# Second layer's experts: the 16 smallest in groups of four instead of two, and one-hot products in bursts of four

## The chip, the cores and the metric

One NeuronCore of a Trainium2 chip runs the whole program. The metric is the device time of one execution in microseconds. Three runs of the kernel before gave 2965.05 us at the median (2964.98 to 2975.44).

## The reference

The reference is a network of three layers on 512 tokens of width 1024, in float32. The first two layers (`first_block`) each end in a mixture of experts. Only the second of these is touched by the change. What it computes:

```
g_idx = argmax(h @ grp_w + grp_b)                     # one of 4 groups per token
e_logit = (h @ exp_w + exp_b)[the 8 experts of that group]
top_v, top_i = top_k(e_logit, 2)                      # two experts of 32 per token
w = g_prob * softmax(top_v)
y[e] = (silu(x[e] @ w_gate[e]) * (x[e] @ w_up[e])) @ w_down[e]     # 1024 -> 512 -> 1024
out[token] = sum over its two experts of w * y[e][token]
```

So 512 tokens make 1024 (token, expert) rows, spread unevenly over 32 experts. Every expert has three weight matrices of 2 MB in float32, 6 MB together; all 32 are read once, 192 MB.

## The kernel before

The expert stage of a layer is `moe`. A router first works out, on VectorE (DVE), each token's two experts, their weights, and each row's position within its expert. Experts 0 and 1 are always the first block. The other 30 are ranked by their number of tokens (`places`), and the list of experts in rank order (`order_list`) is written to memory, where the queue that issues the weight loads (SyncE, SP) reads it into registers (`ranked_expert`).

A block has 128 slots, one for each row of a tile. In the second layer `FIRST = 2` and `MANY = 4`: block 0 holds experts 0 and 1 with 64 slots each; blocks 1 to 4 ("singles") hold one expert each, the four with the most tokens, with 128 slots; the 26 others go in 13 pairs with 64 slots each. That is 18 blocks. The list `turn` gives the order in which they run: the first pair, then a single and three pairs by turns. Rows that don't fit into their expert's slots go to a loop (`overflow`) that stands behind block 12 in turn and whose body runs only if there is such a row.

A block runs through `expert`: its 128 rows are gathered from memory (an indirect DMA on GpSimd, POOL), transposed on TensorE (PE) into `xt`, then multiplied by gate and up (8 row chunks of 128 each, accumulated), activated, transposed into `ht`, and multiplied by down. In a pair the two experts' products stand on the two halves of PE's columns (`tile_position` 0 and 64), so that they can run at once. A float32 product shows as two instructions in the trace. The weights come in tiles of 128 x 1024 float32 (512 KB), 12 to an expert, 384 in all, through a ring of 28 buffers that are used strictly in turn (`raw`, `turn_of`): a load waits until PE is done with the tile that was there 28 tiles ago. Loads are issued by SP in the order gate of block e, down of block e-1, up of block e; PE's order is fixed by hand in the same way (`pe_turn`, `pe`).

The result of a block is added to the residual X by one-hot products: `own_parts` scales the block's output and splits it into a high and a low part, and `add_own` multiplies, for each of 8 column chunks, both parts by a one-hot matrix of the rows' tokens and adds the product to X on DVE. These are slipped in between the expert products of the next blocks: `expert` calls `hooked` after each group of loads (4 calls for gate, 4 for up, 4 for down), and each call takes one step of `add_own`, so two one-hot products over the full array.

After the last block its `add_own` is handed on to the feed-forward part of the third layer, which starts with it.

Of the kernel before, what the change touches and what calls it, by code (L numbers as in the profile page):

```python
# [14 lines left out]
I32 = DT.int32  # L15
AF = mybir.ActivationFunctionType
ALU = mybir.AluOpType
# [8 lines left out]
NE = 32  # L26
NX = 15

FIRST = (2, 2)
MANY = (8, 4)  # L30
Q_LORA, KV_LORA = 384, 256
BIG = 1 << 20
SEGS = [(0, 512), (512, 256)]
# [26 lines left out]
class Kernel:  # L60
# [607 lines left out]
    def places(self, l, pool, tt):  # L668


        V = self.nc.vector
        oh, pos, _, cnt = self.choice
        V.tensor_copy(cnt, self.pc[:, :NE])
        mk = lambda name, *s, dt=F32: pool.tile([128, *s], dt, name="p" + name)
        n1 = FIRST[l] + MANY[l]
        key = mk("key", NE)
        V.scalar_tensor_tensor(key, cnt, float(NE), self.order0[:, l], op0=ALU.mult, op1=ALU.add)
        gt, rank = mk("gt", NE, NE), mk("rank", NE)
        V.tensor_tensor(gt, key.unsqueeze(1).to_broadcast([128, NE, NE]), key.unsqueeze(2).to_broadcast([128, NE, NE]), ALU.is_gt)
        V.tensor_reduce(rank, gt, axis=AX.X, op=ALU.add)  # L680
        oxr, rk = mk("ox", tt, 2, NE), mk("rk", tt, 2)
        V.tensor_tensor(oxr, oh, rank.unsqueeze(1).unsqueeze(1).to_broadcast([128, tt, 2, NE]), ALU.mult)
        V.tensor_reduce(rk, oxr, axis=AX.X, op=ALU.add)
        g, gi, odd, slot = mk("g", tt, 2), mk("gi", 2, tt, 2, dt=I32), mk("odd", 2, tt, 2), mk("slot", tt, 2)
        V.tensor_scalar(g, rk, float(n1), 0.0, op0=ALU.subtract, op1=ALU.max)
        V.tensor_copy(gi[:, 0], g)
        V.tensor_scalar(gi[:, 1], gi[:, 0], 1, None, op0=ALU.arith_shift_right)
        V.tensor_scalar(gi[:, 0], gi[:, 0], 1, None, op0=ALU.bitwise_and)
        V.tensor_copy(odd, gi)

        V.tensor_tensor(g, rk, g, ALU.subtract)
        V.tensor_tensor(g, g, odd[:, 1], ALU.add)
        n = MANY[l] + (NE - n1) // 2
        n += n % 2
        ohb = mk("ohb", tt, 2, n)
        V.tensor_tensor(ohb, self.iota[:, FIRST[l]:FIRST[l] + n].unsqueeze(1).unsqueeze(1).to_broadcast([128, tt, 2, n]),
                        g.unsqueeze(3).to_broadcast([128, tt, 2, n]), ALU.is_equal)

        V.tensor_scalar(g, rk, float(n1), -64.0, op0=ALU.is_ge, op1=ALU.mult)
        V.scalar_tensor_tensor(g, g, 128.0, pos, op0=ALU.add, op1=ALU.is_le)  # L700
        V.scalar_tensor_tensor(slot, odd[:, 0], 64.0, pos, op0=ALU.mult, op1=ALU.add)
        V.scalar_tensor_tensor(slot, g, float(BIG), slot, op0=ALU.mult, op1=ALU.add)
        self.ranked = (gt, rank)
        return ohb, slot

    def order_list(self, l, pool, p2):

        V = self.nc.vector
        gt, rank = self.ranked
        V.tensor_tensor(gt, rank.unsqueeze(1).to_broadcast([128, NE, NE]),  # L710
                        self.iota[:, :NE].unsqueeze(2).to_broadcast([128, NE, NE]), ALU.is_equal)
        V.tensor_tensor(gt, gt, self.iota[:, :NE].unsqueeze(1).to_broadcast([128, NE, NE]), ALU.mult)
        f = p2.tile([128, NE], F32, name="pord")
        V.tensor_reduce(f, gt, axis=AX.X, op=ALU.add)
        self.order = pool.tile([1, NE], I32, name="pordi")
        V.tensor_copy(self.order, f[0:1])
        self.cap = pool.tile([128, NE], F32, name="pcap")
        V.tensor_scalar(self.cap, rank, float(FIRST[l] + MANY[l]), -64.0, op0=ALU.is_ge, op1=ALU.mult)
        light = p2.tile([128, NE], F32, name="plight")
        V.tensor_scalar(light, rank, float(FIRST[l]), -64.0, op0=ALU.is_lt, op1=ALU.mult)  # L720
        V.scalar_tensor_tensor(self.cap, self.cap, 128.0, light, op0=ALU.add, op1=ALU.add)

# [119 lines left out]
    def moe(self, l, n_tok, fg, side_work):  # L842
# [3 lines left out]
        V = nc.vector  # L846
        X = self.X
        tt = n_tok // 128
# [5 lines left out]
        with ExitStack() as st:  # L854
# [4 lines left out]
            with ExitStack() as st1:  # L859
                self.rings.append((st1.enter_context(tc.tile_pool(name=f"raw{l}", bufs=self.more_raw[l], reuse_waits="tile")), self.more_raw[l], None))  # L860
                wsp, n = self.wrings[0][:2]
                self.rings += [(wsp, n, None, "wh"), (wsp, n, None, "wl")]
                with ExitStack() as st2:
# [75 lines left out]
                    self.router(l, lt, pool, p2, n_tok)  # L939
                    oh, pos, v3, _ = self.choice  # L940
                    n1 = FIRST[l] + MANY[l]
                    nb = 1 + MANY[l] + (NE - n1) // 2

                    def lists(name, one_hot, place, bufs):
                        n = one_hot.shape[-1]
# [9 lines left out]
                    one, place, none = [p2.tile([128, tt, 2], F32, name=x) for x in ("fone", "fplace", "fnone")]  # L955
# [10 lines left out]
                    self.order_list(l, pool, p2)  # L966
                    srow, stok, swt = [lambda b, x=x, y=y: y[:, b - 1:b] if b else x for x, y in zip(first, later)]

                turn = [0]
                apart = (nb - 1 - MANY[l]) // MANY[l]  # L970
                for i in range(nb - 1 - MANY[l]):
                    single = [1 + i // apart] * (i % apart == 0 and i // apart < MANY[l])
                    turn += single + [1 + MANY[l] + i]
                pair = n1 - 2 * (1 + MANY[l])
                ranks = lambda b: [0, 1] if b == 0 else [b + 1] if b <= MANY[l] else [2 * b + pair, 2 * b + pair + 1]
                ysc = []
                with ExitStack() as st2:
                    p2 = st2.enter_context(tc.tile_pool(name=f"moee{l}", bufs=1, reuse_waits="tile"))
# [76 lines left out]
                    adds = iter(())  # L1055
# [9 lines left out]
                    for e in range(nb):  # L1065
                        if e == 0:
                            with tc.issue_after(last.ins), tc.issue_after(after_q):
                                next(ex[e])
                        else:
                            if e == own[1] and not direct:  # L1070
                                self.hook = (1, rows)
                            self.pe_turn = direct or e >= own[1]
                            next(ex[e])
                        if e + 1 < nb:
                            start(e + 1)
                        if e:
                            pss = next(ex[e - 1])
                            if direct:
                                for _ in adds:
                                    pass  # L1080
                                adds = add_own(parts_of(e - 1, pss, self.own))
                                self.hook = (1, adds)
                            elif e == own[1]:
                                mine = parts_of(e - 1, pss, p2.tile([128, n_tok], F32R, name="own", tag="ey", bufs=self.eys))
                                self.hook = (2, rows)
                            else:
                                put(e - 1, self.rows_of(p2, pss, swt(turn[e - 1])))
                                if e == own[0]:
                                    next(rows)
                        next(ex[e])  # L1090
                        if e == 2:
                            with tc.issue_after(self.split_last):
                                self.extra(pool)
                            if not direct:

                                z = p2.tile([128, 2, D], F32, name="zero", tag="yr", bufs=2)[:, 0]
                                nc.gpsimd.memset(z, 0.0)
                                for i in own:
                                    put(i, z)
                        if e == self.pause:  # L1100
                            for _ in adds:
                                pass
                            self.hook, self.pe_turn = None, False
                            self.overflow(l, n_tok, h2d, Yd, p2, xg[(e + 2) % 3], add if direct else None)
                            self.pe_last = None
                        if e >= 4:
                            for _ in range(2):
                                next(side_work, None)
# [6 lines left out]
                    if direct:  # L1115
                        adds = add_own(parts_of(nb - 1, pss, self.own, self.turn_of(self.wrings)[0]))
                    else:
                        adds = add_own(mine, parts_of(nb - 1, pss, p2.tile([128, n_tok], F32R, name="own2", tag="ey", bufs=self.eys), p2))
# [18 lines left out]
                    self.fence()  # L1137
        return s

    hook = None  # L1140

    def hooked(self):
        if self.hook:
            for _ in range(self.hook[0]):
                next(self.hook[1], None)

    def pe(self, f, *a, **kw):

# [34 lines left out]
    def expert(self, pool, l, es, x, queue=None):  # L1183
# [16 lines left out]
            else:  # L1200
                nc.scalar.activation(d, v, AF.Copy)
        yield
        parts = [(slice(0, 128), {})] if len(es) == 1 else [(slice(c, c + 64), {"tile_position": (0, c)}) for c in (0, 64)]
        h = pool.tile([128, 512], F32, name=self.uid("eh"), tag="eh", bufs=2)
        for name in ("exp_w_gate", "exp_w_up"):
            ps = self.bank()
# [1194 lines left out]
```

## Time and profile before

| | us |
|---|---|
| median of 3 runs | 2965.05 |
| profiled execution | 2964.15 |
| its span, first to last instruction | 2962.5 |
| PE busy over the span | 2758.8 (93%) |
| DVE busy | 1353.9 (46%) |
| ACT busy | 886.7 (30%) |
| POOL busy | 411.0 (14%) |
| weight tiles read by the two expert stages | 768 of 512 KB |

The profile is of one execution. PE's busy time counts matmuls that overlap as one stretch, so 93% does not say that PE runs at its peak. The second layer's experts lie between about 1278 and 1817 us of the span.

### The profile page before, as it was taken

Reading aid. Unit: us, or ns where it says so; the run is one execution under the profiler, and the core shown is the slowest. Engines: PE = TensorE matmul, PEld = TensorE weight load, DVE = VectorE, ACT = ScalarE, POOL = GpSimd, SP = SyncE. Lnnn points to the kernel's source line nnn. Section 1 sums busy time; section 2 is a strip of 40 time slices with the busy share of each in tenths; the row PEclk is TensorE's granted clock in tenths of the full one; section 3 lists DMA queues with packets and bytes.
Section 4 is the critical chain, followed back from the end, with each engine's and each line's share of the span. In section 5 each row is a group of like instructions: output and inputs, shape, how many; then the busy total and the mean of one; then the engine's idle time right before and its main releaser. Section 6 shows DMA issues by size and latency. Waiting matters only on the chain. (4 is left out here: it accounts for less than half of the span.)

```text
span 2962.5 us, 35613 instructions
## 1 busy us (share of the span) xinstructions
PE 2758.8 (93%) x12938; PEld 1803.1 (61%) x12938; DVE 1353.9 (46%) x2423; ACT 886.7 (30%) x1421; POOL 411.0 (14%) x408
## 2 busy tenths in 40 slices
PE   7989799999988999979999998999999889999998
PEld 4757644333325888833333333788888667888886
DVE  4883520000035576744333334654336777444335
ACT  3563211110103577300000002223225666332223
POOL 1772210000001000010000000650003230000000
PEclk9999899999999999989999999999999999999999
DMA  7666599999994101389999894343334422333331
GB/s 258 210 204 211 219 389 406 399 398 404 398 411 170 63 26 60 115 351 403 372 394 362 335 417 145 104 119 103 97 93 126 135 51 82 97 96 100 93 94 63
DMA packets 207685, 634.63 MB, mean 214 GB/s; under 512 B 29808, under 2 KB 39120, under 8 KB 206736
## 3 DMA queue, kind: packets, MB, share of 16 engines
q1 hardware_dynamic: 194208, 598.89, 55.7%
q0 software_dynamic: 13296, 33.41, 3.1%
q8 instruction: 103, 1.69, 0.2%
q14 instruction: 78, 0.64, 0.1%
HBM read 619.12 MB, written 26.71 MB: 218 GB/s over the span
## 5 line engine op out<-in xcount | busy, mean ns | idle before, releaser
L1152 PE MATMUL ps<-raw,xt 128*64 128x512 f32 (+1 forms) x2048 | 593.4, 608 | 12.0 <-DMA raw<-exp_w_up 8.4
L169 PE MATMUL ps<-Hh,wh 128*128 128x512 f32 (+1 forms) x1320 | 495.2, 381 | 3.5 <-ACT Hh L262 2.1
L171 PE MATMUL ps<-Hh,wl 128*128 128x512 f32 (+1 forms) x1320 | 495.7, 377 | 2.9 <-DVE wl L91 2.9
L170 PE MATMUL ps<-Hl,wh 128*128 128x512 f32 (+1 forms) x1320 | 497.9, 378 | 0.2 <-DVE Hl L263 0.2
L89 ACT ACTIVATE wh<-raw 128x1024 fp32r<-128x1024 f32 (+1 forms) x224 | 231.6, 1040 | 582.5 <-PE ps L170 477.6
L1152 PEld LDWEIGHTS ps<-raw,xt 128*64 128x64 f32 (+1 forms) x2048 | 189.1, 148 | 329.9 <-issue 269.4
L91 DVE TENSOR_TENSOR wl<-raw,wh 128x1024 fp32r<-128x1024 f32 (+1 forms) x224 | 276.2, 1237 | 204.8 <-ACT wh L89 204.5
L1152 PE MATMUL ps<-raw,ht 128*64 128x512 f32 (+1 forms) x1024 | 281.1, 597 | 29.1 <-DVE ht L1225 26.3
L169 PEld LDWEIGHTS ps<-Hh,wh 128*128 128x128 f32 x1320 | 248.5, 189 | 67.9 <-issue 5.0
L170 PEld LDWEIGHTS ps<-Hl,wh 128*128 128x128 f32 x1320 | 249.2, 189 | 55.4 <-issue 4.2
L171 PEld LDWEIGHTS ps<-Hh,wl 128*128 128x128 f32 x1320 | 248.5, 189 | 51.0 <-DVE wl L91 3.8
L1218 DVE TENSOR_TENSOR eh<-ps,eh 128x512 f32<-128x512 f32 x38 | 26.3, 692 | 417.5 <-PE ps L1152 377.9
L1152 PEld LDWEIGHTS ps<-raw,ht 128*64 128x64 f32 (+1 forms) x1024 | 100.2, 146 | 188.9 <-issue 146.3
L1029 DVE SCALAR_TENSOR_TENSOR X<-ps,mod,X 128x512 f32<-128x512 f32 (+1 forms) x160 | 116.7, 736 | 190.2 <-PE ps L1152 190.1
L1216 ACT ACTIVATE eh<-ps 128x512 f32<-128x512 f32 x38 | 22.7, 597 | 478.3 <-PE ps L1152 478.2
L413 POOL TENSOR_TENSOR cg<-cg,cp 128x798 f32<-128x798 f32 x60 | 121.8, 2030 | 95.7 <-ACT cp L412 87.6
L985 POOL DMA_INDIRECT xg<-h2d,stok x36 | 36.2, 1005 | 515.4 <-PE ps L1152 464.2
L169 PE MATMUL ps<-Gh,wh 128*128 128x512 f32 x256 | 101.1, 395 | 0.0
L171 PE MATMUL ps<-Gh,wl 128*128 128x512 f32 x256 | 101.1, 395 | 0.0
L170 PE MATMUL ps<-Gl,wh 128*128 128x512 f32 x256 | 101.1, 395 | 0.0
L1571 DVE TENSOR_TENSOR fs<-ps,fs 128x512 f32<-128x512 f32 x44 | 30.4, 691 | 142.6 <-PE ps L171 141.9
L1152 PEld LDWEIGHTS ps<-own,ysh 128*128 128x128 f32 x152 | 28.4, 187 | 95.7 <-issue 93.0
(741 smaller groups left out, 4153.7 us busy)
## 6 DMA issues: line engine op xcount, KB each, us to landing
raw<-exp_w_gate SPq DMA_DIRECT2D x256, 512.0 KB
raw<-exp_w_up SPq DMA_DIRECT2D x256, 512.0 KB
raw<-exp_w_down SPq DMA_DIRECT2D x256, 512.0 KB
raw<-ffn_w SPq DMA_DIRECT2D x132, 512.0 KB
raw<-mod_w SPq DMA_DIRECT2D x96, 512.0 KB
X<-xT SPq DMA_DIRECT2D x16, 384.0 KB
raw<-w_in_ab SPq DMA_DIRECT2D x12, 512.0 KB
yr<-yd POOLq DMA_DIRECT2D x6, 1024.0 KB, 8.3
```

The source lines that it names most:

```text
L89: self.nc.scalar.activation(dst.hi, src, AF.Copy)
L91: self.split_last = eng.tensor_tensor(dst.lo, src, dst.hi.bitcast(F32), ALU.subtract).ins
L169: mm(ps, a.hi, b.hi, start=start, stop=False)
L170: mm(ps, a.hi, b.lo, start=False, stop=False)
L171: mm(ps, a.lo, b.hi, start=False, stop=stop)
L413: nc.gpsimd.tensor_tensor(a, a, t, ALU.add)
L985: nc.gpsimd.indirect_dma_start(out=x, out_offset=None, in_=h2d, in_offset=bass.IndirectOffsetOnAxis(ap=stok(turn[e]), axis=0), bounds_chec ...
L1029: V.scalar_tensor_tensor(xs, ps[:, :c], self.mcol(l, 5, k, i), xs, op0=ALU.mult, op1=ALU.add)
L1152: i = f(*a, **kw).ins
L1216: nc.scalar.activation(h, ps, AF.Silu)
L1218: nc.vector.tensor_tensor(h, ps, h, ALU.mult)
L1571: V.tensor_tensor(s, ps, s, ALU.mult)
```

## The change

The second layer gets a third kind of block. `FEW = (0, 16)`: of the ranked experts the last 16 get 32 slots each and run four to a block, on quarters of PE's columns (`tile_position` 0, 32, 64 and 96). The ten experts of ranks 6 to 15 stay in 5 pairs. That makes 1 + 4 + 5 + 4 = 14 blocks. `places` works out the new slots, `order_list` the new number of slots per expert for the overflow test. The order in `turn` becomes: the first pair, then a four and a single, four times, then the five pairs. In the first layer `FEW` is 0, and its blocks and their order are as before.

The hook that adds the one-hot products takes two steps at every second call instead of one step at each: four one-hot products in a row, half as often.

```diff
+FEW = (0, 16)
 # places
+        n2 = NE - FEW[l]
         V.tensor_scalar(g, rk, float(n1), 0.0, op0=ALU.subtract, op1=ALU.max)
+        if FEW[l]:
+            f, fi, quarter = mk("f", tt, 2), mk("fi", 2, tt, 2, dt=I32), mk("quarter", 2, tt, 2)
+            V.tensor_scalar(f, rk, float(n2), 0.0, op0=ALU.subtract, op1=ALU.max)
+            V.tensor_tensor(g, g, f, ALU.subtract)
+            V.tensor_copy(fi[:, 0], f)
+            V.tensor_scalar(fi[:, 1], fi[:, 0], 2, None, op0=ALU.arith_shift_right)
+            V.tensor_scalar(fi[:, 0], fi[:, 0], 3, None, op0=ALU.bitwise_and)
+            V.tensor_copy(quarter, fi)
...
+        if FEW[l]:
+            V.tensor_tensor(g, g, f, ALU.subtract)
+            V.tensor_tensor(g, g, quarter[:, 1], ALU.add)
-        n = MANY[l] + (NE - n1) // 2
+        n = MANY[l] + (n2 - n1) // 2 + FEW[l] // 4
...
+        if FEW[l]:
+            V.tensor_scalar(f, rk, float(n2), -32.0, op0=ALU.is_ge, op1=ALU.mult)
+            V.tensor_tensor(g, g, f, ALU.add)
...
+        if FEW[l]:
+            V.scalar_tensor_tensor(slot, quarter[:, 0], 32.0, slot, op0=ALU.mult, op1=ALU.add)
 # order_list
+        if FEW[l]:
+            V.tensor_scalar(light, rank, float(NE - FEW[l]), -32.0, op0=ALU.is_ge, op1=ALU.mult)
+            V.tensor_tensor(self.cap, self.cap, light, ALU.add)
 # moe
-                    nb = 1 + MANY[l] + (NE - n1) // 2
+                    n2 = NE - FEW[l]
+                    nb = 1 + MANY[l] + (n2 - n1) // 2 + FEW[l] // 4
...
+                one = list(range(1, 1 + MANY[l]))
+                two = list(range(1 + MANY[l], 1 + MANY[l] + (n2 - n1) // 2))
                 turn = [0]
-                apart = (nb - 1 - MANY[l]) // MANY[l]
-                for i in range(nb - 1 - MANY[l]):
-                    single = [1 + i // apart] * (i % apart == 0 and i // apart < MANY[l])
-                    turn += single + [1 + MANY[l] + i]
-                pair = n1 - 2 * (1 + MANY[l])
-                ranks = lambda b: [0, 1] if b == 0 else [b + 1] if b <= MANY[l] else [2 * b + pair, 2 * b + pair + 1]
+                for b in [*range(1 + MANY[l] + len(two), nb), *two]:
+                    turn += [one.pop(0), b] if one and (not FEW[l] or len(turn) > 1) else [b]
+                turn = [*turn[:-1], *one, turn[-1]]
+                pair, four = n1 - 2 * (1 + MANY[l]), n2 - 4 * (nb - FEW[l] // 4)
+                ranks = lambda b: ([0, 1] if b == 0 else [b + 1] if b <= MANY[l] else
+                                   [2 * b + pair + i for i in range(2)] if b in two else [4 * b + four + i for i in range(4)])
...
-                                self.hook = (1, adds)
+                                self.hook = (2, adds, 2)
 # hooked
-            for _ in range(self.hook[0]):
-                next(self.hook[1], None)
+            n, g, *every = self.hook
+            self.beat += 1
+            if self.beat % (every or [1])[0] == 0:
+                for _ in range(n):
+                    next(g, None)
 # expert
-        parts = [(slice(0, 128), {})] if len(es) == 1 else [(slice(c, c + 64), {"tile_position": (0, c)}) for c in (0, 64)]
+        n = 128 // len(es)
+        parts = [(slice(c, c + n), {} if n == 128 else {"tile_position": (0, c)}) for c in range(0, 128, n)]
```

## Rows read from the trace of the kernel before

**Rows 1.** Timeline of ACT and PE, end of the stage: start us, us, engine, line.
```profile
1816.53 1.52 ACT L1012 ACTIVATE wh<-ps,swt 128x512 fp32r<-128x512 f32 x2 [19.63 <-PE ps L1152]
1824.78 1.05 PE L169 MATMUL ps<-Hh,wh 128*128 128x512 f32 x2
```

**Rows 2.** Windows: window, length, busy PE PEld DVE ACT POOL, granted clock, DMA share, GB/s.
```profile
1278.00:1797.00 519.00, 490.79 (x1954) 190.71 (x1956) 183.13 (x321) 35.42 (x53) 16.86 (x17) 0.99 0.97 381
1676.00:1780.00 104.00, 99.50 (x398) 36.75 (x396) 36.65 (x56) 7.29 (x11) 0.00 (x0) 1.00 1.03 416
1300.00:1340.00 40.00, 37.73 (x146) 16.87 (x144) 13.56 (x21) 2.57 (x4) 2.96 (x3) 1.00 1.03 416
1260.00:1280.00 20.00, 5.43 (x32) 4.82 (x30) 18.36 (x82) 1.92 (x4) 2.72 (x2) 0.63 0.51 180
840.00:860.00 20.00, 15.04 (x48) 4.27 (x45) 4.80 (x8) 0.00 (x0) 1.75 (x3) 0.91 1.03 414
```

**Rows 3.** Waits of PE, 1281 to 1820: total us, times, longest us.
```profile
PE ps L1152 <- DVE ht L1225: 25.5, 18, 1.9
```

**Rows 4.** Waits of SP's queue, 1280 to 1800: total us, times, longest us.
```profile
SPq L133 <- PE ps L1152: 194.3, 164, 19.2
...
SPq L793 <- DVE xli L780: 1.9, 1, 1.9
```

**Rows 5.** Chain of waits, two pairs: start us, us, what.
```profile
1729.70 27.22 PE ps L1152 x112
...
1760.00 27.22 PE ps L1152 x112
```

**Rows 6.** Timeline of PE: a down projection, pair chunks, single chunks.
```profile
1402.04 7.09 PE L1152 MATMUL ps<-raw,ht 128*64 128x512 f32 x32 [1.50 <-DVE ht L1225]
...
1411.44 1.94 PE L1152 MATMUL ps<-raw,xt 128*64 128x512 f32 x8
...
1413.97 1.94 PE L1152 MATMUL ps<-raw,xt 128*64 128x512 f32 x8
...
1418.94 1.88 PE L1152 MATMUL ps<-raw,xt 128*128 128x512 f32 x4
...
1421.12 1.88 PE L1152 MATMUL ps<-raw,xt 128*128 128x512 f32 x4
```

**Rows 7.** Timeline of SP's queue: the issue of tiles (xN of them).
```profile
1276.27 1.95 SPq L133 DMA_DIRECT2D raw<-exp_w_gate  x4
...
1294.78 9.00 SPq L133 DMA_DIRECT2D raw<-exp_w_gate  x8
...
1343.05 10.67 SPq L133 DMA_DIRECT2D raw<-exp_w_up  x8
...
1641.67 2.62 SPq L133 DMA_DIRECT2D raw<-exp_w_gate  x4
...
1683.34 9.08 SPq L133 DMA_DIRECT2D raw<-exp_w_gate  x8
...
1774.34 9.69 SPq L133 DMA_DIRECT2D raw<-exp_w_down  x8
1794.46 46.19 SPq L133 DMA_DIRECT2D raw<-ffn_w  x8
```

**Rows 8.** Four-quarter products elsewhere: those running at 24.2 us; timeline at 1830.80.
```profile
L362 PE MATMUL ps<-raw,sc x4: 1062/1062/1062, 24.2 to 24.2; 128*32 128x512 f32 x4
...
1830.80 1.06 PE L1152 MATMUL ps<-x,gs 128*32 128x512 f32 x6
```

**Rows 9.** Timeline of DVE: the ordered list is written.
```profile
1275.61 0.17 DVE L716 CAST pordi<-pord 1x32 int32<-1x32 f32 x1
```

**Rows 10.** DMA queues, 1280 to 1800: packets, MB, share of 16 engines.
```profile
DMA packets 55603, 197.87 MB, mean 381 GB/s; under 512 B 7367, under 2 KB 7367, under 8 KB 55570
...
q0 software_dynamic: 2448, 4.02, 2.1%
```

**Rows 11.** SP at the branch of the overflow loop: both layers, first and last start.
```profile
L794 SPq COMPARE_BRANCH x2: 45/49/53, 674.2 to 1621.8; - x2
```

**Rows 12.** The page's first line.
```profile
span 2962.5 us, 35613 instructions
```

More of the change, by code (lines that the diff above doesn't have):

```diff
@@ L1138, in moe @@
         return s
-    hook = None
+    hook, beat = None, 0
     def hooked(self):
         if self.hook:
-            for _ in range(self.hook[0]):
-                next(self.hook[1], None)
+            n, g, *every = self.hook
[3 more added lines that the diff above has]
+                    next(g, None)
     def pe(self, f, *a, **kw):
```

## The prediction

> **What bounds the kernel now.** I first looked for the stretch that the edit touches: the second layer's experts, from the first gathered block near 1278 us to the eviction of the last one at 1816.53 [rows 1]. The windows view gives PE busy 490.79 of 519 us and a mean of 381 GB/s over it [rows 2]. So two resources are nearly full, and the question is which one waits for the other. The waits view settles it: PE's longest wait in the stretch is for DVE's copy of `ht`, 25.5 us in 18 pieces, once per block [rows 3], and no expert tile appears among PE's waits; SP, which issues the tiles, waits 194.3 us for PE to free buffers [rows 4]. PE is late, the DMA is held back. The chain of waits says the same: two pairs in a row start their third piece at 1729.70 and 1760.00, and what lies between is PE plus about 3 us of DVE at the hand-over [rows 5]. A pair costs 30.3 us.
>
> A sum over blocks confirms it. On the PE timeline a chunk of a pair (8 instructions of 64 columns, two running at once, plus one one-hot visit) takes 1413.97 - 1411.44 = 2.53 us, a chunk of a single 1421.12 - 1418.94 = 2.18 us; a down projection takes 7.09 us for 32 instructions, so one slot is 0.433 us [rows 6]. A single is 8 x 2.18 + 7.1 + 3.3 (transposes and hand-over) = 27.8 us. Before: 14 pairs x 30.3 + 4 singles x 27.8 = 535 us; seen, from the restart near 1283 to 1816.53, 533 us.
>
> How fast could the DMA go? While SP was issuing without a pause, 72 tiles of 512 KB (nine groups of eight) went from 1683.34 to 1774.34 [rows 7]: 91.0/72 = 1.264 us each, at 416 GB/s and a DMA share of 1.03. The stretch 1300 to 1340 has the same 416 GB/s and 1.03 at an earlier, different place [rows 2], so I take that as the ceiling. A pair's 24 tiles need 30.3 us, which equals PE's pace; a single's 12 need 15.2 us against PE's 27.8. The lost DMA time is in the singles and in a stop before 1641.67, where SP waited 19.2 us for PE [rows 4, 7].
>
> **The change part by part.**
>
> *18 blocks become 14.* The 26 experts of rank 6 and up were 13 pairs; now there are 5 pairs and 4 fours. The order is pair, then four and single four times over, then five pairs. All 384 tiles are still loaded. A four runs the same number of array slots as a pair if four 32-column products run at once. The trace has that form elsewhere: at 24.2 us four products of 128x32 are in flight together, and at full clock six such records span 1.06 us, which is two slots and the tail of one [rows 8]. So a chunk of a four is 4 slots, 1.73 us, and its block about 29 us of PE, while its 48 tiles take 48 x 1.264 = 60.7 us. PE's total becomes about 6 x 29.4 + 4 x 27.8 + 4 x 29 = 404 us. PE leaves the path and the DMA takes it.
>
> *DMA sum.* The first load of the second block is issued at 1276.27, when 16 of the 384 tiles have been issued [rows 7]; that waits for the ordered list, written at 1275.61 [rows 9]. Remaining: 368 x 1.264 = 465.2 us. Gathers share the engines: the software queue has 2.1% of the 520 us window, 10.9 us [rows 10], and moves the same 1024 token rows afterwards, so I keep 10.9. First landing about 2 us after issue (estimate; the wait pieces on the DMA are 1 to 2 us). Last tile: 1276.3 + 2 + 465.2 + 10.9 = 1754.4, or 1.29 us a tile with the gathers in it.
>
> *PE behind the last tile.* After a four PE is level with the tiles. The last single puts it behind by at most 27.8 - 15.5 = 12 us, spread over its neighbours some 9; each of the five pairs takes 24 x 1.29 = 31.0 us of DMA against 29.4 of PE and gives back 1.6. That leaves 2 us, plus a few at the overflow branch: 6 us. Bounds: 2 (the last chunk alone) and 10 (nothing given back).
>
> *Bursts.* A visit costs 2.53 - 4 x 0.433 = 0.80 us in a pair but 2.18 - 4 x 0.433 = 0.45 in a single, whose products use the whole array like the one-hot ones; the 0.35 us is the change of array form [rows 6]. Four visits fewer per block save 1.4 us of PE; the second addition to X at the hand-over (0.75 us on DVE, partly overlapped) gives back about 0.5. So a pair is 29.4. It matters only at the end, as above; 14 blocks instead of 18 also drop 64 one-hot products, off the path now.
>
> *The overflow branch* stands after block 12 in turn in both versions. SP passes it at 1621.8 without stopping [rows 11]; its first load behind it then waited the 19.2 us, because the body that is not run takes 12 of the 28 buffers in turn, so that load needs the tile 16 back, not 28 back, to be done. With SP waiting for buffers all along, PE was then nearly the whole ring behind. With PE under 10 us (8 tiles) behind, this stall goes: 0 us, at worst 5. What is late next is the DMA itself.
>
> *Longer router.* `places` has eleven more small DVE instructions and `order_list` two, near 0.17 us each with issue [rows 9]. Most of them lie beside or behind the list that SP waits for; SP then reads four registers per four instead of two. On the path: 0.5 us, between 0 and 13 x 0.17 = 2.2. PE's first product moves by as much, hidden by the loads. SP's read of the overflow list stands in the same queue and waited 1.9 us [rows 4]; beside the tiles in flight it costs 0, at worst 5.
>
> *Does a token fall out of 32 slots?* Routing the reference's drawn inputs, the 16 smallest experts of layer two hold at most 30 tokens, ranks 6 to 15 at most 49. The overflow body stays unrun.
>
> *The tail.* The first FFN tiles are issued at 1794.46, 22 us before PE is done [rows 1, 7]; now they land only a few us before. Their two splits may then stand in the way of the last evictions: 1.5 us, between 0 and 4. Layer one and all else are unchanged.
>
> *Sum.* PE ends at 1754.4 + 6 + 0.5 = 1761 instead of 1816.5: -55.5; tail +1.5: -54. The profiled execution took 2964.15 us (span 2962.5 [rows 12]) and would take 2910; the median, 2965.05, is 0.9 above it: **2911 us**. With all low ends (no gather cost, PE 2 behind, no tail): 1276.3 + 2 + 465.2 + 2 = 1745.5, -71, 2894. With a tile at the pace between 1294.78 and 1343.05 (36 tiles in 48.3 us, 1.34 each, gathers within) [rows 7]: 368 x 1.34 = 493, PE end 1777.5 + 0.5, tail 4: 2931.
>
> **The rivals.**
> *The clock falls in the fours.* PE now waits for tiles. When it was busy 5.43 of 20 us the granted clock was 0.63, at 15.04 of 20 it was 0.91 [rows 2]. In a four, products start tile by tile: two slots after each of the first three tiles, four after the last, 4.3 of 5.2 us per chunk, so I expect near 1. At the lower level (1.2 GHz, a slot twice as long) a four's PE time is about 12 x 3.5 + 8 x 1.2 + 4 = 56 us, still under its loads, but the singles then find no slack, and each four and single together need 56 + 27.8 = 84 us against 77: four times 7 is 28 us, 2939. The Trainium skill ("TensorE: Matmul & The Clock Gate", Loop structure matters more than you think) speaks for this: waiting for a DMA between bursts of products makes PE run slow. By that rule the sum would be these 2939 us; the trace's 0.91 lies nearer to mine.
> *The DMA does not go faster.* If four experts' streams kept the mean of 381 GB/s, the window's 197.87 MB [rows 10] would take 519 us as now; only PE's part behind the last tile shrinks: 1278 + 519 + 6 = 1803, 2953 us. Against it: 416 GB/s over 104 us, with pairs.
> *Slower: quarters one after another.* If each of the four products of a row chunk waited for the one before, a chunk would be 16 slots, 6.9 us, a four 12 x 6.9 + 8 = 91 us, over its 61 us of loads; then PE binds again: 4 x 91 + 4 x 27.8 + 6 x 29.4 = 652 us, end 1936, 3085 us. It decides from two at a time downward: at two a four is 50 us and stays under its loads. Against it: the four records in flight together.
>
> **How the numbers follow.** Forecast 0.79, slow clock 0.12, no faster DMA 0.06, serial quarters 0.03. About 0.5% (15 us) is what a measurement can tell from no change, so faster means under 2950: forecast, slow clock and a third of the third case, 0.93; same 0.04; slower 0.03. The range runs from 2894 to 2938: the forecast with both ends and most of the slow clock's case.
>
> **What would show it.** Right: in the changed profile PE's waits in the stretch are for `exp_w_*` tiles, SP's for PE nearly vanish, DMA stays at 1.03 and 416 GB/s from 1280 to about 1750, four 128x32 records start together, and the FFN's first product moves from 1824.78 [rows 1] to about 1771. Wrong: GB/s near 390 with PE waiting (ceiling misread), a granted clock under 0.8 in the fours, 6 to 7 us per chunk of a four, or a long SP wait at the branch.

## The result and the profile after

The changed kernel takes 2923.02 us (median of 4 runs, 2919.81 to 2926.05) against 2965.51 (4 runs, 2964.98 to 2975.44): a ratio of 0.9849, 95% interval 0.9826 to 0.9872. The prediction was 2911, within 2894 to 2938. The sign and the mechanism came out; 12 us of the gain did not.

All of the gain lies in the second layer's expert stage. Its end on ACT and the FFN's first product, which stood at 1816.53 and 1824.78 [rows 1], in the timelines of the changed kernel (start us, us, engine, line):

```profile
1775.22 1.53 ACT L1037 ACTIVATE wh<-ps,swt 128x512 fp32r<-128x512 f32 x2 [18.95 <-PE ps L1180]
...
1784.13 1.05 PE L171 MATMUL ps<-Hh,wh 128*128 128x512 f32 x2
```

That is -41.3 us where -55.5 was forecast, and 0.7 us given back in the tail where 1.5 was. From the FFN on both kernels take the same: 2962.5 - 1824.78 = 1137.7 us before, 2921.4 - 1784.13 = 1137.3 after.

The waits of SP's queue in the changed kernel, 1280 to 1790 (total us, times, longest us):

```profile
SPq L135 <- DMA raw<-exp_w_down: 94.8, 124, 2.8
SPq L135 <- DMA raw<-exp_w_gate: 89.4, 116, 2.0
SPq L135 <- DMA raw<-exp_w_up: 88.2, 118, 2.1
SPq L135 <- PE ps L1180: 13.1, 43, 0.8
```

SP used to wait 194.3 us for PE [rows 4] and 117 us for its own transfers; now it waits 272 us for its own transfers and 13 for PE, and the 19.2 us at the overflow branch are gone. The bound has moved from PE to the loads, as forecast. A four whose tiles are all there, on PE's timeline:

```profile
1305.21 7.07 PE L1180 MATMUL ps<-raw,xt 128*32 128x512 f32 x64 [0.35 <-DVE xt L1224]
```

These are 64 quarter products, 16 slots if four run at once: 7.07/16 = 0.442 us a slot, against 0.433 [rows 6]. So the rival of serial quarters is out. The windows view (length, busy PE PEld DVE ACT POOL, granted clock, DMA share, GB/s):

```profile
1300.00:1340.00 40.00, 36.74 (x191) 11.64 (x188) 6.68 (x10) 3.38 (x5) 1.97 (x2) 1.00 1.03 408
1340.00:1400.00 60.00, 54.21 (x225) 20.45 (x225) 25.79 (x67) 2.57 (x4) 1.97 (x2) 0.97 1.03 407
1460.00:1560.00 100.00, 90.20 (x367) 31.59 (x366) 25.10 (x41) 4.54 (x7) 2.96 (x3) 1.00 1.03 408
1676.00:1740.00 64.00, 60.48 (x270) 24.20 (x268) 24.19 (x37) 3.95 (x6) 0.00 (x0) 1.00 1.02 407
```

In these windows, three of which hold fours, the granted clock is 0.97 to 1.00, so the slow clock is out too. The last column is what was not expected: the same DMA share of 1.02 to 1.03 as before, but 407 to 408 GB/s and not 416 [rows 2].

### The profile page after: what moved, and what is told of

Read it like the earlier page. It is cut to its first block, busy times and chain, and to the rows that moved or that the text cites. A ratio compares the mean times of both kernels' runs of the same rounds, so it can differ in the third digit from the quotient of the medians.

```text
span 2921.4 us, 35291 instructions
## 1 busy us (share of the span) xinstructions
PE 2709.3 (93%) x12826; PEld 1783.5 (61%) x12826; DVE 1310.1 (45%) x2372; ACT 878.8 (30%) x1409; POOL 405.8 (14%) x404
## 3 DMA queue, kind: packets, MB, share of 16 engines
q1 hardware_dynamic: 194208, 598.89, 55.5%
## 5 line engine op out<-in xcount | busy, mean ns | idle before, releaser
L1180 PE MATMUL ps<-raw,xt 128*64 128x512 f32 (+2 forms) x2048 | 571.4, 607 | 21.5 <-DMA raw<-exp_w_up 13.8
L1180 PEld LDWEIGHTS ps<-raw,xt 128*64 128x64 f32 (+2 forms) x2048 | 181.4, 141 | 364.0 <-issue 237.5
L1180 PE MATMUL ps<-raw,ht 128*64 128x512 f32 (+2 forms) x1024 | 275.1, 616 | 28.9 <-DVE ht L1254 20.6
L1180 PEld LDWEIGHTS ps<-raw,ht 128*64 128x64 f32 (+2 forms) x1024 | 93.9, 142 | 192.7 <-issue 130.3
L1054 DVE SCALAR_TENSOR_TENSOR X<-ps,mod,X 128x512 f32<-128x512 f32 (+1 forms) x128 | 88.1, 729 | 152.8 <-PE ps L1180 152.8
L422 DVE SCALAR_TENSOR_TENSOR cv<-U,cw,cv 128x512 f32<-128x512 f32 x120 | 76.2, 635 | 3.1
```

Of the source, the lines that this page charges most:

```text
L422: V.scalar_tensor_tensor(s, u, cw[:, g, j:j + 1], s, op0=ALU.mult, op1=ALU.add)
L1054: V.scalar_tensor_tensor(xs, ps[:, :c], self.mcol(l, 5, k, i), xs, op0=ALU.mult, op1=ALU.add)
L1180: i = f(*a, **kw).ins
```

## The experiments

Whole times of one kernel scatter by 5 to 15 us, and the second block's first tile is issued anywhere between 1276 and 1284 in these profiles, in both kernels (1267 in e7, for a reason told there). So each run is also judged by its **stage length**: from that issue to the first eviction of the last block. It is 1816.53 - 1276.27 = 540.3 us before [rows 1, 7] and 1775.22 - 1279.63 = 495.6 us after. Ratios are to the kernel before.

**Is 416 GB/s the kernel's or that execution's?** The kernel before again, unchanged.

> The kernel before, unchanged, profiled beside the other runs of this batch. It tells whether the 416 GB/s that its first profile showed at 1300 to 1340 and 1676 to 1780 us belong to the kernel or to that execution; the changed kernel's profile has 407 GB/s in the same stretches at the same DMA share of 1.02. If the ceiling differs from execution to execution (or from chip to chip): the two stretches show some other rate here, and the other profiles of this batch show the same one in their starved stretches, within 3 GB/s. If the ceiling is lower in the changed kernel because of what it does (four experts' tiles in flight side by side, another order of experts): 416 again here and 407 again in the changed kernels of this batch.

2969.74 us, stage length 540.0. The windows view:

```profile
1300.00:1340.00 40.00, 38.60 (x149) 16.65 (x145) 10.38 (x15) 3.85 (x5) 1.98 (x2) 1.00 1.03 417
1676.00:1740.00 64.00, 61.00 (x240) 23.65 (x238) 20.74 (x32) 3.95 (x6) 0.00 (x0) 1.00 1.03 417
```

The rate belongs to the kernel. The changed kernels of the same batch show 408 in the first window (e2 and e4, the latter with pairs there, not fours), so four experts side by side are not the reason either.

**Bursts taken back, and bursts alone.** In the changed kernel, and in the kernel before:

```
-  self.hook = (2, adds, 2)
+  self.hook = (1, adds)        # e2; e3 is the reverse, in the kernel before
```

> The changed kernel with the one-hot products given out one visit per chunk again, as in the kernel before; fours stay. A visit costs a block of column groups about 0.35 us more than a single's, so 4 x 0.35 = 1.4 us of PE per block, less some 0.5 us of the second addition: 0.9 us. Theory A (the loads set the pace until the last tile, and PE ends some 8 us behind it, a lag made by the last single and worked off in the last five pairs at 31.6 us of loads against 29 of PE): only the last single and the five pairs count, 6 x 0.9 to 6 x 1.4, so +5 to +8 us against the changed kernel, 2928 to 2931. Theory B (PE sets the pace all along): 14 x 0.9 = +13 us or more. Theory C (the loads alone set the end): 0 to +1 us.

> The kernel before with bursts alone: two visits on every second chunk, pairs and singles as they were, 18 blocks. There PE sets the pace, so each of the 14 pairs should save what a burst saves on PE. By the prediction's 0.9 us (four visits fewer x 0.35, less 0.5 at the hand-over) 14 x 0.9 = -13 us, about 2953; if nothing is given back at the hand-over, 14 x 1.4 = -20 us, 2946. Rival: the one-hot visits cost PE nothing that isn't hidden, or the pairs are held by the loads (24 x 1.264 = 30.3 us, which equals PE's pace), so 0 to -3 us, 2962 to 2965. What it shows is the part of the -42 us that the edit of the bursts alone brings.

Without bursts 2922.69 us, ratio 0.9846 (0.9830 to 0.9861), the same as with them; stage length 498.2. Theory C in the whole time, half of A in the stage: the bursts carry next to nothing here. Alone they bring 0.9968 (0.9956 to 0.9981), -9.5 us, stage length 535.0; -13 was the prediction's price. In the profiled run, too, the stage is only 5.0 us shorter than in e1. The last pairs of the kernel before give nothing: their gate tiles are issued 1719.01 - 1688.84 = 30.17 us apart without bursts (e1) and 1718.39 - 1688.23 = 30.16 with them (e3), the pace of 24 tiles at 417 GB/s.

**A four last.** 

```
+  turn = [0, *range(5, 10), 1, 10, 2, 11, 3, 12, 4, 13]
```

> The changed kernel with its blocks in another order: the five pairs come right behind block 0 and the stage ends with single, four, single, four, ... and last a four, whose tiles take twice PE's time. Theory A (PE ends 8 us behind the last tile because singles make a lag that the pairs work off only slowly): PE ends about 2 us behind, so -6 us against the changed kernel; up to 3 us of it lost, because a four's last chunk needs four tiles: -3 to -6, 2917 to 2920. Theory B (PE sets the pace): 0. A loss of over 3 us would mean that order itself costs something, for example the overflow block's place among the tiles.

2919.83 us, ratio 0.9839 (0.9824 to 0.9854), too close to 0.9849 to call; stage length 494.7, -0.9. Theory A wanted -3 to -6. So whatever lies behind the last tile, little of it is a lag that singles make and pairs work off; how much is read from the tiles' completions below.

**What the tile buffers' addresses do.** One more difference between the kernels touches a transfer: where it lands. Tiles go through 28 buffers in turn. By the program's own allocation, 17 of them moved from 87552 to 87456, since the router's lists ahead of them have one column a block, rounded up to 14 instead of 18, and so became 96 bytes smaller; the other 11 start 32 above a multiple of 64 in both kernels. Three paddings of the changed kernel, and one of the kernel before:

```
+  if l == 1: pool.tile([128, 24], F32, name="pad")   # e5: 96 bytes; e6: [128, 8], 32 bytes
                                                       # e8: 32 bytes, kernel before
   # e7: 8 floats in front of every ring, 24 more in layer one, 16 more in layer two
```

> The changed kernel with 96 unused bytes per partition in front of the second layer's 17 extra tile buffers. The longer list code, whose tiles are allocated ahead of them, is 96 bytes smaller than before, so those 17 of the 28 buffers that expert tiles go through moved from address 87552 to 87456 (from a multiple of 256 to 32 above a multiple of 64); the other 11 start 32 above a multiple of 64 in both kernels. This puts the 17 back to 87552 and changes nothing else. Theory A (a tile costs more DMA time where its buffer does not start on a boundary): the starved stretches at 1300 to 1340 and 1676 to 1740 show 416 to 417 GB/s instead of 407 to 408, a tile 1.26 instead of 1.285 us, 368 x 0.025 = -9 us, 2914. Theory B (the lower rate comes from more tiles in flight, or from PE, DVE and the DMA meeting otherwise): 408 GB/s and 2923 us as in the changed kernel.

> The same with 32 unused bytes: the 17 buffers start at 87488, a multiple of 64 but 192 above a multiple of 256. If a boundary of 64 bytes is what counts: 416 GB/s and 2914 us, as in the run with 96 bytes. If it is one of 256: the rate stays at 405 to 409, 2923 us. The Trainium skill (DMA: Bandwidth & Descriptors, How a descriptor splits into AXI transactions) says that a transaction must start from a 256-byte boundary and that the bytes between that boundary and the start still cost beats of 32 bytes: by it 4096 bytes would take 128 beats at a multiple of 256, 133 at the changed kernel's 87456, 134 here, 135 in the other 11 buffers; that is 130.8 on the mean before, 133.8 after and 134.4 here, so 405 GB/s here by the 407 of after.

> The changed kernel with unused bytes ahead of every ring of tile buffers, in both layers, so that all buffers start on a multiple of 256 (32 bytes ahead of the common 11, 96 ahead of the first layer's 13, 64 ahead of the second's 17). Theory A: if 28 shifted buffers take 1.285 us a tile (408 GB/s) and 17 aligned with 11 shifted 1.260 (416), an aligned one takes (28 x 1.260 - 11 x 1.285)/17 = 1.244 us: 421 GB/s in the second layer's starved stretches, 368 x 0.041 = -15 us against the changed kernel, of which PE, whose pairs take 29 to 29.4 us against 30 of loads then, may keep some 3. In the first layer 11 of 24 buffers gain: 384 x 11/24 x 0.041 = -7 us if the loads set its pace (its profile shows a DMA share of 1.02). So 2900 to 2911. Theory B: 2923. The Trainium skill (the same section) would have 128 beats everywhere against 133.8 on the mean: 407 x 133.8/128 = 425 GB/s.

> The kernel before with 32 unused bytes ahead of the second layer's 17 buffers: 87584 instead of 87552, so that all 28 start 32 above a multiple of 64, as in the changed kernel. Theory A: the stretches at 1300 to 1340 and 1676 to 1740, at 416 to 417 GB/s in three profiles of that layout, show 407 to 410; its time rises by 0 to 8 us, since PE sets part of the pace there. Theory B: 416 to 417 again.

The same window of the four, e5 to e8 in this order:

```profile
1300.00:1340.00 40.00, 36.76 (x193) 11.15 (x190) 6.68 (x10) 1.97 (x3) 1.98 (x2) 1.00 1.03 415
```
```profile
1300.00:1340.00 40.00, 36.48 (x190) 10.84 (x187) 6.68 (x10) 1.97 (x3) 1.98 (x2) 1.00 1.03 407
```
```profile
1300.00:1340.00 40.00, 37.12 (x145) 13.04 (x142) 8.63 (x13) 2.57 (x4) 0.99 (x1) 1.00 1.02 418
```
```profile
1300.00:1340.00 40.00, 38.61 (x150) 16.86 (x148) 10.38 (x15) 3.85 (x5) 1.97 (x2) 1.00 1.03 409
```

In this window theory A holds in all four. Moved back by 96 bytes, the rate is 415 again; on a multiple of 64 that is none of 256 it stays at 407; the kernel before, pushed off, falls from 417 to 409. The Trainium skill (DMA: Bandwidth & Descriptors, How a descriptor splits into AXI transactions) has the rule, told of what a transaction fetches, while here the buffer written to was moved. An estimate from its beats puts the kernel before at 407 x 133.8/130.8 = 416, as measured, and e6 at 405, where the trace has 407. It doesn't fit the other two: e7 would have 425 and has 418; in e8 the 17 buffers are only 32 bytes off, which makes 129 beats, 131.4 on the mean and so 414 GB/s, and the trace has 409. What the runs show is the boundary itself: with all buffers off it, the 17 by 32, 160 or 192 bytes, the rate is 407 to 409. In the second stretch that the expectations name, 1676 to 1740, e8 has 408 and e6 405, but e5 has 391 and e7 409: there SP waits for PE (9.2 us in e5), so that window doesn't show the loads' own rate.

In time: e5 2916.14 us, 0.9826 (0.9808 to 0.9845), stage length 490.7 (-4.9 for a forecast of -9; the loads alone end 8.2 us sooner, as the completions below show, but SP now waits 24 us for PE instead of 13). The interval of its ratio overlaps that of the changed kernel. e6 2924.99 us, 0.9862 (0.9840 to 0.9885), 495.7; of the two, which differ by 64 bytes of padding, every run of e5 (up to 2918.23) is faster than every run of e6 (from 2921.25). e8 2970.71 us, 540.0: PE sets the pace there, so the rate costs nothing. e7 2914.81 us, 0.9824 (0.9804 to 0.9843): stage length 486.2, and the first layer's experts, from the first copy of `h` to the next stage's first weight, take 545.7 us instead of 554.3: -9.4 and -8.6, for a forecast of -12 to -15 and -7. But 7 us are lost again in the last FFN, which takes 371.1 us from its first product to its last against 364.1 in e5. Its windows in e7 and in e5:

```profile
2550.00:2600.00 50.00, 50.00 (x216) 40.27 (x215) 21.80 (x27) 14.34 (x17) 0.00 (x0) 1.00 0.30 95
```
```profile
2550.00:2600.00 50.00, 50.00 (x222) 41.43 (x221) 23.22 (x28) 15.06 (x19) 0.00 (x0) 1.00 0.30 95
```

PE is busy throughout at clock 1.00 in both, yet passes 216 products and not 222; every other profile here has 222 or 223. Why is open: e7 is the only run that moved the buffers of split weights, and nearly everything else, by 32 bytes, but it is one profile, and that move wasn't tried alone.

**One transfer moved into the idle gap.** 

```
+  if early:                                    # block 0, ahead of the list
+      held = [[self.raw(v[:, k]) for v in [self.ew("exp_w_down", l, e) for e in es]] for k in range(4)]
```

> The changed kernel with one transfer moved: the eight down tiles of block 0 (whose experts don't depend on the sort) are issued ahead of SP's wait for the sorted list, instead of behind the second block's 16 gate tiles. In the changed kernel's profile SP issues nothing between 1267 and 1279.63, while it waits 12.4 us for that list, and the DMA runs empty there. Theory A (the loads set the pace of the whole stage, so a tile that lands in the gap is a tile less later): 8 tiles x 1.285 = 10 us of transfers move into the gap, less what the copies of h and the buffers still in use keep: -6 to -10 us, 2913 to 2917. Theory B (PE sets the end, 8 us behind the last tile, and keeps its own order): 0 to -2 us, 2921 to 2923.

2927.22 us, ratio 0.9866 (0.9845 to 0.9887), stage length 498.2: no gain, +2.7 in the stage. Both theories missed. Its windows view and its waits (of PE, then SP):

```profile
1260.00:1280.00 20.00, 4.45 (x28) 3.83 (x28) 18.50 (x93) 2.40 (x5) 0.00 (x0) 0.65 1.00 384
1280.00:1300.00 20.00, 13.99 (x58) 7.11 (x60) 6.95 (x21) 0.00 (x0) 6.11 (x6) 0.67 0.71 222
```
```profile
PE ps L1180 <- DMA xg<-h2d,ftok: 5.0, 1, 5.0
...
SPq L135 <- PE ps L1180: 41.6, 50, 13.9
```

The gap did fill: 384 GB/s between 1260 and 1280, where the changed kernel has 201. But the copies of `h` stand in the same queue between the down tiles; the last is issued near 1273, not 1267, so block 0's rows come 5 us late, PE frees no buffer, and with 24 of 28 in use SP stands still for up to 13.9 us: 222 GB/s from 1280 to 1300 instead of 361. What was moved forward was given back.

**PE's work taken away.** No one-hot products and additions for 13 of the 14 blocks.

```
-  adds = add_own(parts_of(e - 1, pss, self.own)); self.hook = (2, adds, 2)
+  adds = iter(()); self.hook = None
```

> The changed kernel without the one-hot products and the additions to X of all second-layer blocks but the last (13 of 14 blocks leave them out, so their contribution is missing from the output). It takes 13 x 32 products of 0.23 us, near 97 us at full pace, and their array changes off PE, and 13 x 16 additions off DVE; loads and expert products stay. Theory A (the loads set the pace; PE's lag behind the last tile is all that PE still adds): the lag of 8 us falls to the last chunk's 2, so -5 to -8 us, 2915 to 2918, the DMA rate stays at 407 to 408 GB/s. Theory B (PE's total still counts): -30 us and more.

The expectation counts too much: a block has 8 chunks with two products and one addition each, so 13 blocks leave out 208 products (the changed kernel's trace has them in the stage, e10's has none) and 104 additions. At 0.23 us each, about half of a visit in a single [rows 6], that is an estimated 48 us of PE, and not 97.

2924.93 us, ratio 0.9858 (0.9843 to 0.9874), stage length 494.8: -0.8 us for some 48 us of PE. Theory B is out, and A's -5 to -8 doesn't come either. Part of the freed time, 14.7 us, turns up as waits of PE for tiles, 30.2 us in 120 pieces instead of 15.5 in 57:

```profile
PE ps L1181 <- DMA raw<-exp_w_up: 11.5, 49, 0.9
PE ps L1181 <- DMA raw<-exp_w_down: 9.5, 30, 0.8
PE ps L1181 <- DMA raw<-exp_w_gate: 9.2, 41, 0.2
```

PE's busy time in the stage falls by only 11.7 us, from 454.8 to 443.1: the expert products left start further apart, and as PE's busy time counts what overlaps once, the same 512 gate and up products of the fours take up 119.8 us of it instead of 106.4.

**The gains together, and the FFN's tiles held back.** e11 is e4, e5, the early down tiles and the first layer's 13 buffers on 256. e12 leaves out the early tiles, and starts the ring 14 places later:

```
+  self.rings[0][2][0] += 14 * (FEW[l] > 0)
```

> The changed kernel with the second layer's 17 buffers back on 87552, the first layer's 13 extra buffers moved from 83328 to 83456 (from 128 above a multiple of 256 to a multiple of 256), the stage's order ending with a four, and block 0's down tiles issued ahead of the list. If the gains add up: -7 (measured for the second layer's buffers) -3 (a four last) -6 to -10 (early down tiles) and -2 to -4 in the first layer (13 of 24 buffers, where putting all 24 on 256 brought its end forward by 10 us): -18 to -24 us, 2899 to 2905. If with faster loads PE binds instead, its 404 us of blocks and its hand-overs leave less: -10 to -14 us, 2909 to 2913.

> The changed kernel with the second layer's buffers back on 87552, the first layer's 13 on a multiple of 256, a four last (as in earlier runs, without the early down tiles), and one new edit: the second layer's ring of 28 starts 14 places later, so that its last five expert tiles lie in the five buffers that the FFN's first tiles use. Those FFN tiles are then issued only when PE is done with the last expert tiles, not 10 us before. In the changed kernel the five FFN tiles are in flight together with the last eight expert tiles (issues 1763.0 and 1764.25, the DMA busy until 1774.5). Theory A (tiles in flight share the DMA, so the FFN's five keep the last expert tiles from landing): from the issue of the second block's first tile to the eviction of the last block, 495.6 us in the changed kernel, 490.7 with the buffers moved, 494.7 with a four last, comes to 490 - 5 x 1.26 = 484; the first FFN product stays 8 to 10 us behind the eviction; 2903 to 2907 in all. Theory B (tiles land in the order of issue, the last expert tile at 1768, and what follows is PE): 489 to 490 us again, the FFN's product 1 to 3 us later, 2909 to 2912.

e11: 2910.46 us, 0.9802 (0.9788 to 0.9815), stage length 489.2; less than the sum, since the early tiles cost again (SP waits 15.5 us for PE once). The time lies in the range forecast for a PE that binds, but its last tile lands only 1.1 us before the eviction, so that isn't the reason. e12: 2907.75 us, 0.9801 (0.9785 to 0.9816), stage length 486.8, the first layer's experts 550.2 us; both beat the changed kernel. 486.8 lies between theory A's 484 and B's 489. What decides is the end, where nothing follows the last tile any more, in the windows of e12 and on its PE:

```profile
1754.00:1756.00 2.00, 2.00 (x9) 0.82 (x8) 1.17 (x2) 0.00 (x0) 0.00 (x0) 1.00 1.03 412
1756.00:1758.00 2.00, 1.77 (x12) 0.41 (x11) 0.24 (x1) 0.00 (x0) 0.00 (x0) 1.00 0.67 262
1758.00:1760.00 2.00, 1.78 (x9) 0.38 (x5) 0.00 (x0) 0.00 (x0) 0.00 (x0) 1.00 0.14 55
```
```profile
1757.33 2.31 PE L1184 MATMUL ps<-raw,ht 128*32 128x512 f32 x12 [0.23 <-DMA raw<-exp_w_down]
1759.87 1.05 PE L1184 MATMUL ps<-raw,ht 128*32 128x512 f32 x2 [0.22 <-DMA raw<-exp_w_down]
1761.15 1.05 PE L1184 MATMUL ps<-raw,ht 128*32 128x512 f32 x2 [0.23 <-DMA raw<-exp_w_down]
1762.42 1.90 PE L1184 MATMUL ps<-raw,ht 128*32 128x512 f32 x10 [0.23 <-DMA raw<-exp_w_down]
```

The DMA falls from a share of 1.03 through 0.67 to 0.14, while PE still waits for one tile every 1.27 us, the last until 1762.42. The trace says more. It keeps sixteen completions for every tile, as many as there are DMA engines, and a tile counts only with the last of them. The last expert tile of e12 is issued at 1752.29, with nothing behind it; fifteen of its parts are in between 1756.71 and 1759.73, the sixteenth at 1762.38, 10.1 us after the issue and 0.04 us before PE goes on. In e4, with FFN tiles behind it, the last tile is issued at 1760.50, has fifteen parts by 1766.89 and the sixteenth at 1770.57, again after 10.1 us. So A's sharing is out; and B is out as well, since PE waits for transfers. One part in sixteen, read as one engine's, is late, and it holds up more than the end: in the changed kernel SP issues 95% of the tiles 0.12 us after the sixteenth part of the tile eight before. The Trainium skill (DMA: Bandwidth & Descriptors, Latency and other measured facts) knows two engines that are usually slower, and guesses at the software queue's descriptors; here one part is late, the rows don't tell whose it is, and these tiles go through the hardware queue.

The sixteenth part of the last expert tile also splits every stage length in two, with one profile a row:

| | loads: first issue of the stage to the last tile complete, us | from there to the eviction, us |
|---|---|---|
| before | 517.3 | 23.0 |
| changed kernel | 493.5 | 2.1 |
| e4, four last | 493.6 | 1.1 |
| e10, no additions | 493.6 | 1.2 |
| e6, buffers on 64 | 493.6 | 2.1 |
| e5, buffers back on 256 | 485.3 | 5.5 |
| e7, all on 256 | 483.3 | 2.9 |
| e12 | 485.7 | 1.1 |

The loads take the same 493.5 to 493.6 us whatever the order and however little PE has to do, and 8 to 10 us less with the buffers on 256; in e5, which ends with pairs, 3.4 us of that go back to PE at the end. e12's gain over e5 lies there, with a four last, and not in its loads: holding back the FFN's tiles bought nothing.

## Why the prediction held, and where the 14 us went

**Right.** What bounds the stage before and after; the quarters four at a time; the branch's stall gone (SP's wait there 0.5 us); the clock (0.97 to 1.00, with 15.5 us of waits for tiles, 1.7 us at the longest); layer one unchanged (554.8 us before, 554.3 after); the longer router. For that last step: from the logits on DVE to the written list it takes 20.0 us in one and 20.9 to 21.0 in three profiles of the old router, 20.2 in six and 21.1 in four of the new, so +0.2 where 0.5 was taken. The second block's first tile came 3.4 us later in this profile, but that is the scatter of what lies ahead of the stage (1276.27, 1281.57, 1282.72 and 1282.90 with the old router).

**The failed step is the DMA sum's tile.** The prediction took 1.264 us a tile "as the ceiling", read from two places of the trace. The number was right, and again 417 in the repeat; but it was a property of 17 buffer addresses, and the change moves those by making the router's lists smaller. At 408 GB/s a tile takes 0.5243 MB/408 = 1.285 us: 368 x 0.021 = +7.7 us. Nothing in the trace of before could show this, though the program's allocation could.

The sum has a second gap. It lets a tile be complete when its bytes are through, but the last expert tile is complete 493.5 us after the first issue, where the sum has 1754.4 - 1276.3 = 478.1. Of these 15.4 us the rate makes 7.7. The tiles' bytes were through, on the mean of the DMA engines, 1768.0 - 1279.6 = 488.4 us after the first issue. This is read from the hardware queue's 192.56 MB from 1279 to 1767, 0.38 MB short of 368 tiles:

```profile
q1 hardware_dynamic: 52872, 192.56, 99.6%
```

368 x 1.285 + 10.9 + 2 = 485.8 leaves +2.6, most of it the slow first 20 us (361 GB/s). The other 5.1 us, from 1768.0 to 1773.1, are the late sixteenth part: the other fifteen of the last expert tile are in by 1768.7. With +2.9 for the later start (3.4 less the 0.5 counted) and 2.1 instead of 6 us of PE behind the last tile, so -3.9, that is 14.4 of the 1775.2 - 1761 = 14.2 us.

**Right size, wrong cause.** From the point where the bytes are through to the eviction it takes 7.2 us, near the 6 of the prediction, but that is luck: 5.1 are the late part, which the prediction doesn't have, and 2.1 are PE's. The lag itself was rightly argued. In the changed kernel PE's last wait for an expert tile ends at 1606.15, so in all five pairs it is behind the tiles, and the pairs work that off; but 2.1 us are left and not 6, and without 48 us of PE's work still 1.2. Likewise the bursts: of the 13 us that "0.9 us a pair" makes, e3 shows 9.5 in the whole time and 5.0 in the stage, where PE binds, and e2 next to nothing where it doesn't, as the text said of the end.

**Still open.** Why full alignment gives 418 and not more, why 32 bytes off cost as much as 160, why the last FFN passes fewer products in e7, and which DMA engine is late and why.

## What to carry to other kernels

When a stage becomes bound by its loads, a rate read from the trace of before holds only as long as the buffers stay where they are: compare the start addresses of the tile buffers in both programs, and put them on multiples of 256 bytes. Multiples of 64 (e6) didn't do, nor did 128: e12 moved the first layer's 13 buffers from 128 above a multiple of 256 to one, and its experts took 550.2 us instead of 554.3. A transfer that moves into an idle gap must be weighed with all that queues behind it and with the buffers it holds; here the rows of the first block and a full ring took back the whole 10 us. To tell what is really behind the last tile, take one engine's work away altogether, and read when the last part of that tile lands.

## What the hardware showed that was not expected

- 4 KB rows written to buffers off a 256-byte boundary cost rate at an unchanged DMA share: 407 to 409 GB/s at 1300 to 1340 with all 28 buffers off it, 17 of them by 32, 160 or 192 bytes alike, 415 to 417 with 17 on it, 418 with all on it.
- Of the sixteen parts of a 512 KB tile one is late: fifteen are in 5.7 us after the issue of the changed kernel's last expert tile, the sixteenth after 10.1; in e12, with nothing behind it, 7.4 and 10.1.
- Four 32-column products at once lose almost nothing: 0.442 us a slot of four, against 0.433 for a slot of two halves.
- With all buffers shifted by 32 bytes PE passed 216 instead of 222 products in 50 us, fully busy and at the same granted clock of 1.00 (one profile; the cause is not shown).
